# Products for eight tokens in two-bank PSUM tiles, and lists with fewer VectorE steps, in a hybrid decoder layer with expert retrieval

## The chip, the cores and the metric

The kernel runs on one core of one Trainium2 chip. A core has TensorE (PE, matmuls), VectorE (DVE), ScalarE (ACT), GpSimd (POOL) and SyncE (SP), each with its own queue of instructions that it works through in order, and 16 DMA engines that fill on-chip memory (SBUF). TensorE writes to PSUM, eight banks here, which VectorE and ScalarE read. The metric is the time of one execution on the device in microseconds.

## The reference

One decoder layer over 512 prompt tokens and 32 sample tokens, width 1024: retention and a convolution share a projection in and a projection out, a layer norm follows, and then an expert retrieval (PEER), whose sum is added to the tokens ahead of a second layer norm. The retrieval is what the change touches:

```python
q = (xb @ w_query).reshape(PEER_BLOCK, PEER_HEADS, PEER_DQ)          # 8 heads, 256
q1, q2 = q[..., : PEER_DQ // 2], q[..., PEER_DQ // 2:]
s1 = jnp.einsum('phd,hkd->phk', q1, sub_keys_1)                       # 128 keys
s2 = jnp.einsum('phd,hkd->phk', q2, sub_keys_2)
v1, i1 = lax.top_k(s1, PEER_TOPK)                                     # 16
v2, i2 = lax.top_k(s2, PEER_TOPK)
cand = (v1[..., :, None] + v2[..., None, :]).reshape(PEER_BLOCK, PEER_HEADS, PEER_TOPK * PEER_TOPK)
sv, ci = lax.top_k(cand, PEER_TOPK)
e1 = jnp.take_along_axis(i1, ci // PEER_TOPK, axis=-1)
e2 = jnp.take_along_axis(i2, ci % PEER_TOPK, axis=-1)
idx = e1 * N_KEYS + e2
gate = jax.nn.softmax(sv.astype(jnp.float32), axis=-1).astype(xb.dtype)
u = jnp.take(peer_u, idx, axis=0)                                     # of 16384 experts
act = jax.nn.gelu(jnp.einsum('phkd,pd->phk', u, xb), approximate=False)
vv = jnp.take(peer_v, idx, axis=0)
return jnp.einsum('phk,phkd->pd', gate * act, vv)
```

So each token has 8 x 16 = 128 experts with a gate each. The matrices are float32.

## The kernel before

The retrieval is computed in two ways. For 288 tokens (the first 128 prompt tokens, the 32 samples, a block b of 128) the rows of u and v of each expert are gathered from memory by GpSimd's indirect DMAs, one expert per token at a time, into a tile of 128 x 2048. Of each gathered tile VectorE takes the dot with the token (line 697), ScalarE the Gelu (708) and the product with the gate (709), and VectorE accumulates (714). For the last 256 tokens (ND) all experts are computed densely, for one "key" e after another, 128 experts each: the scores sp of a key are 8 matmuls (`scores_of`, line 973; the trace lists each twice, so 16), their Gelu goes to a place in the tiles Ga, Gb, Gc and Gd, and this is multiplied by the gate weights of the tokens, which are zero but for their 128 experts.

These gate weights are built on chip. A list (`retrieve`) finds for some heads of up to 128 tokens the 16 best experts E and their gates: VectorE sorts (`top16`), converts positions (622, 623), adds candidates (628), sorts again, finds the experts by comparison (644 to 651), and lines 653 to 658 are the softmax, whose exp alone is on ScalarE and needs its own table there. There are 14 lists: five for the first 128 tokens, four for the 256 dense tokens, one for the samples ("s") and four for block b.

For the dense tokens experts and gates are transposed (line 1021, ScalarE copies 1025 to 1029, VectorE 1031 and 1033 split the gate into two float16 parts gtT). `build` then makes for each group of 8 tokens (TB) an A that marks the first sub-key (odd groups on VectorE, 1070; even ones on ScalarE, 1076 and 1077) and a B that has the gate at the second (VectorE, M at 1080 and twice B at 1084), and multiplies them on TensorE (1100), two matmuls a token, into a PSUM tile of 4 tokens x 96 keys. `first_keys` takes each such tile out: for keys whose Gelu is there already VectorE multiplies it in place (1129), for the others ScalarE copies it (1132). Keys 52 to 95 have their scores ahead of the build (`early_keys`, Gelu at 1005). The other 52 (`s_stage`) are scored between the products, with Gelus at 1113 and 1115 and a product on VectorE for the tokens that have been built (1116). After the tokens of S_AT, 4 in this kernel, list "s" starts behind the last eviction.

Then the V stage: for each key 4 matmuls (1159; 8 in the trace) of the weights with the key's rows of v into the accumulators pB, four PSUM banks. Before it the `residual` (537) puts the scaled tokens into these banks, 16 matmuls (32 in the trace). The last 32 keys are scored, built and multiplied within the V stage. The gathers, the lists of block b, and the norms of the finished blocks run on the other engines all along.

PSUM: the early scores have four banks (psp, banks 4 to 7), the transposes and query products the other four (pq, banks 0 to 3). When both are released, the pool pdn takes two banks for "mm" (products) and two for sp, and pacc the four of pB.

The order of each engine's instructions is set by the tile framework's scheduler, which simulates the program; `behind` adds an order between two instructions. Keys' rows ("uv") are loaded by SyncE into four buffers (UV).

## Time and profile before

| | us |
|---|---|
| median of 3 runs | 1465.27 (1461.19 to 1468.07) |
| the profiled execution | 1464.26 |
| its span | 1462.5 |
| TensorE busy | 1402.5 (96%) |
| VectorE busy | 1166.1 (80%) |
| ScalarE busy | 500.6 (34%) |
| GpSimd busy | 420.1 (29%) |
| DMA engines, mean rate | 347 GB/s, 506.80 MB in all |

The profile is of one execution; the span runs from its first to its last instruction. "Busy" adds the instructions' durations without overlaps. A matmul's end is modelled. A row of a timeline has its start from the span's begin, its length, the engine, the line of the kernel, the operation, what it writes and reads with shapes, how many instructions of the kind followed one another (x), and in brackets how long the engine was idle before it and what is taken to have released it. PEclk is the share of TensorE's full clock that was granted.

### The profile page before, as it was taken

The numbers are of one execution on the slowest core, as the hardware profiler recorded it, in microseconds if no ns is written. First come the engines' busy times: TensorE is split into PE (matmuls) and PEld (weight loads), VectorE is DVE, ScalarE is ACT, GpSimd is POOL, SyncE is SP. The second block draws the span as 40 slices with busy tenths as digits, with TensorE's granted clock in tenths as the row PEclk, the third lists the DMA queues.
The fourth block names the chain that finished last, engine by engine and source line by source line (L and its number), as shares of the span: only waits on it lengthen the run. The fifth ranks groups of instructions, "written<-read, shape, count | busy, mean of one in ns | idle before, by whom it ended". The sixth has DMA issues, their size and how long they took to land. (4 is left out here: it accounts for less than half of the span.)

```text
span 1462.5 us, 19654 instructions
## 1 busy us (share of the span) xinstructions
PE 1402.5 (96%) x6666; PEld 960.8 (66%) x6666; DVE 1166.1 (80%) x2874; ACT 500.6 (34%) x1498; POOL 420.1 (29%) x405
## 2 busy tenths in 40 slices
PE   8898899999999999989999999999999999999997
PEld 7878455568767578878888884444444666666443
DVE  5828878988858989999899996878879766666666
ACT  1423673345122232333545542113655111111111
POOL 1172134333432322232222311333322222222330
PEclk9999999999999999999999999999999999999999
DMA  9849489978989689999999966999999999999995
GB/s 349 307 174 373 171 286 370 413 291 293 347 357 375 223 315 389 364 395 348 328 395 361 347 252 227 423 422 402 386 354 365 398 416 405 418 404 405 410 407 196
DMA packets 100403, 506.80 MB, mean 347 GB/s; under 512 B 10279, under 2 KB 21287, under 8 KB 57413
## 3 DMA queue, kind: packets, MB, share of 16 engines
q0 software_dynamic: 43392, 309.32, 54.1%
q1 hardware_dynamic: 52157, 190.10, 34.0%
q10 hardware_dynamic: 4752, 6.11, 1.2%
q8 instruction: 53, 0.87, 0.2%
q14 instruction: 49, 0.40, 0.1%
HBM read 500.12 MB, written 5.80 MB: 346 GB/s over the span
## 5 line engine op out<-in xcount | busy, mean ns | idle before, releaser
L973 PE MATMUL sp<-x1T,uv 128*128 128x256 f32 x2048 | 463.8, 383 | 0.4 <-ACT Gc L1115 0.2
L973 PEld LDWEIGHTS sp<-x1T,uv 128*128 128x128 f32 x2048 | 386.3, 191 | 65.0 <-issue 11.9
L714 DVE SCALAR_TENSOR_TENSOR acc<-g,wgt,acc 128x1024 f32<-128x1024 f32 x252 | 323.1, 1282 | 69.6 <-ACT wgt L709 68.8
L697 DVE SCALAR_TENSOR_TENSOR g<-g,x 128x1024 f32<-128x1024 f32 x255 | 310.7, 1220 | 64.5 <-DMA g<-in_uv_dram,Ib 41.2
L708 ACT ACTIVATE act<-act 128x1 f32<-128x1 f32 x288 | 57.7, 202 | 593.9 <-DVE g L697 522.3
L691 POOL DMA_INDIRECT g<-in_uv_dram,Ib x126 | 147.1, 1167 | 383.3 <-PE pB L1159 136.9
L691 POOL DMA_INDIRECT g<-in_uv_dram,I x104 | 134.3, 1291 | 318.7 <-DVE acc L714 187.2
L1159 PE MATMUL pB<-uv,Ga 128*128 128x512 f32 x352 | 158.1, 594 | 0.0
L235 PE MATMUL mm<-x1T,w 128*128 128x384 f32 (+1 forms) x448 | 153.6, 501 | 0.0
L235 PEld LDWEIGHTS mm<-x1T,w 128*128 128x128 f32 x448 | 85.1, 192 | 64.1 <-issue 32.6
L1159 PE MATMUL pB<-uv,Gb 128*128 128x512 f32 x256 | 115.6, 606 | 2.3 <-DVE Gb L1129 1.9
L1159 PEld LDWEIGHTS pB<-uv,Ga 128*128 128x128 f32 x352 | 66.1, 190 | 67.5 <-issue 66.0
L1159 PE MATMUL pB<-uv,Gd 128*128 128x512 f32 x256 | 110.0, 592 | 0.0
L1159 PEld LDWEIGHTS pB<-uv,Gb 128*128 128x128 f32 x256 | 47.8, 192 | 67.3 <-issue 52.6
L1159 PEld LDWEIGHTS pB<-uv,Gd 128*128 128x128 f32 x256 | 48.6, 190 | 60.8 <-issue 59.3
L1076 ACT ACTIVATE A<-row,e1T 128x128 f16<-128x128 bf16 x256 | 78.5, 389 | 18.9 <-PE mm L1100 14.6
L1159 PE MATMUL pB<-uv,Gc 128*128 128x512 f32 x160 | 72.2, 600 | 0.4 <-DMA uv<-in_uv_dram 0.4
L235 PE MATMUL mm<-g,w 128*128 128x160 f32 (+1 forms) x512 | 68.0, 294 | 0.0
L235 PEld LDWEIGHTS mm<-g,w 128*128 128x128 f32 x512 | 67.1, 198 | 0.2 <-ACT score L607 0.2
L1113 ACT ACTIVATE W<-sp 128x256 f32<-128x256 f32 (+26 forms) x84 | 26.7, 318 | 118.0 <-PE sp L973 102.6
L1100 PEld LDWEIGHTS <-A 128*128 128x128 f16 x1024 | 43.5, 97 | 31.3 <-issue 12.4
L691 POOL DMA_INDIRECT g<-in_uv_dram,Is x25 | 34.5, 1378 | 80.9 <-DVE acc L714 27.2
(317 smaller groups left out, 1713.6 us busy)
## 6 DMA issues: line engine op xcount, KB each, us to landing
uv<-in_ut_dram SPq DMA_DIRECT2D x128, 512.0 KB
uv<-in_uv_dram SPq DMA_DIRECT2D x128, 512.0 KB
w<-in_w_in_dram SPq DMA_DIRECT2D x18, 1024.0 KB
w<-in_w_query_dram SPq DMA_DIRECT2D x15, 1024.0 KB
w<-in_w_out_dram SPq DMA_DIRECT2D x7, 1024.0 KB
ln<-in_ln_g_dram POOLq DMA_DIRECT2D x5, 512.0 KB
ln<-in_ln_b_dram POOLq DMA_DIRECT2D x5, 512.0 KB
g<-in_uv_dram,Ib POOLq DMA_INDIRECT x126
```

The costliest lines, as they stand in the source:

```text
L235: T.matmul(p[:, :n], w[m // 2][:, k, (m % 2) * 128:(m % 2 + 1) * 128], xT[:, k, c0:c0 + n], start=(k == 0), stop=(k == 7))
L691: fetch = G.indirect_dma_start(out=t, out_offset=None, in_=a["uv"], in_offset=bass.IndirectOffsetOnAxis(ap=idx[:, k:k + 1], axis=0))
L697: dot = V.scalar_tensor_tensor(t[:, :D], t[:, :D], 1.0, x1, op0=OP.mult, op1=OP.mult, accum_out=act[:, 0:1])
L708: S.activation(act[:, 1:2], act[:, 0:1], AF.Gelu)
L714: V.scalar_tensor_tensor(acc, v, wgt, acc, op0=OP.mult, op1=OP.add)
L973: mm = T.matmul(sp[:, i], u[:, k], x1T[:, k, NG2:], start=(k == 0), stop=(k == 7), skip_group_check=True)
L1076: S.activation(A[:, t], row, AF.Abs, bias=e1T[:, t1 + t:t1 + t + 1])
L1100: mm = T.matmul(pt[:, t % nt], A[t % TB], B[:, q, t % TB // 2, :, t % 2], start=(q == 0), stop=(q == 1))
L1113: S.activation(W[:, :n], sp[:, :n], AF.Gelu)
L1159: return [T.matmul(pB[b][q], W[:, b * 128:(b + 1) * 128], vt[:, q * 512:(q + 1) * 512], start=False, stop=(e == NK - 1), skip_group_check= ...
```

## The change

The lists: positions are converted and multiplied by 1 or 128 in one VectorE instruction, with a small constant tile. The candidates' positions are converted to int16 on ScalarE. The softmax loses the subtraction and the sum on VectorE: ScalarE copies the negated maximum, and computes one exp per head with this as its bias and the sum as a second output. The reciprocal and the product with it stay on VectorE.

The build: a PSUM tile has 8 tokens x 128 places (two banks), of which 96 are used, and three such tiles form the pool pbd. The scores get two banks of their own, psc. Each tile is taken out once, so for 8 tokens in one instruction per range of keys; S_AT becomes 8. The pool of the accumulators pB, and the pool pdn which the last 32 keys' products use, are opened when pbd is closed, after `first_keys`; the residual stands there too.

```diff
@@ -41,7 +41,7 @@
 TURN = (90, 92)
-S_AT = 4
+S_AT = 8
 EG = (32, 20, 44, 32)
@@ -203,6 +203,9 @@
     G.iota(row, pattern=[[1, NK]], base=0, channel_multiplier=0, allow_small_or_imprecise_dtypes=True)
+    unit_k = per.tile([128, 2], F32, name="unit_k")
+    G.memset(unit_k[:, 0:1], 1.0)
+    G.memset(unit_k[:, 1:2], float(NK))
     mhalf = per.tile([128, 1], F32, name="mhalf")
@@ -619,8 +622,8 @@
                     later(first)
-        V.tensor_copy(fi[:n], iu[:n])
-        V.tensor_scalar(fi[:n, :, 1], fi[:n, :, 1], float(NK), None, op0=OP.mult)
+        V.tensor_tensor(fi[:n], iu[:n],
+                        unit_k[:n].unsqueeze(1).unsqueeze(3).to_broadcast([n, nh, 2, TK]), op=OP.mult)
         cand = pick("cand", [128, 2, nh, NCAND], bufs=1)
@@ -634,7 +637,7 @@
         ci = pick("ci", [128, nh, NCAND], I16, bufs=1)
-        V.tensor_copy(ci[:n], cand[:n, 1])
+        S.activation(ci[:n], cand[:n, 1], AF.Copy)
         pf = pick("pf", [128, nh, TK, 2], BF)
@@ -649,11 +652,11 @@
             V.tensor_reduce(E[:n, e0 + j:e0 + j + m], oh[:, :, :, 0:14], axis=AX.X, op=OP.add)
-        ex = pick("ex", [128, nh, TK])
-        V.tensor_sub(ex[:n], sv[:n], sv[:n, :, 0:1].to_broadcast([n, nh, TK]))
-        S.activation(ex[:n], ex[:n], AF.Exp)
-        sm = pick("sm", [128, nh])
-        V.tensor_reduce(sm[:n], ex[:n], axis=AX.X, op=OP.add)
+        ex, sm = pick("ex", [128, nh, TK]), pick("sm", [128, 2, nh])
+        S.activation(sm[:n, 1], sv[:n, :, 0], AF.Copy, scale=-1.0)
+        for j in range(nh):
+            S.activation(ex[:n, j], sv[:n, j], AF.Exp, bias=sm[:n, 1, j:j + 1], accum_out=sm[:n, 0, j:j + 1])
+        sm = sm[:, 0]
         V.reciprocal(sm[:n], sm[:n])
@@ -1045,16 +1048,12 @@
-    pdn = ctx.enter_context(tc.tile_pool(name="pdn", bufs=2, space=PSUM, reuse_waits="tile"))
-    psp[:] = [pdn]
+    psp[:] = [ctx.enter_context(tc.tile_pool(name="psc", bufs=2, space=PSUM, reuse_waits="tile"))]
+    pbs = ExitStack()
+    pdn = [pbs.enter_context(tc.tile_pool(name="pbd", bufs=3, space=PSUM, reuse_waits="tile"))]
     sel[:] = [bsel, True]
...
     gc = ctx.enter_context(tc.tile_pool(name="gc", bufs=1, reuse_waits="tile"))
-    pacc = ctx.enter_context(tc.tile_pool(name="pacc", bufs=1, space=PSUM, reuse_waits="tile"))
-    pB = [[pacc.tile([128, 512], F32, name=f"pB{b}{q}") for q in range(2)] for b in range(2)]
-    for b in range(2):
-        for q in range(2):
-            residual(pB[b][q], x1T, range(q * 4, q * 4 + 4), NG2 + b * 128)
     GW[1] = gc.tile([128, EG[1], ND], F32, name="Gc")
@@ -1094,7 +1093,7 @@
                 if t % nt == 0:
-                    pt = pdn.tile([128, nt, ne], F32, name="mm")
+                    pt = pdn[0].tile([128, nt, ne if ahead else 128], F32, name="mm")[:, :, :ne]
                 A, B = ready[t // TB]
@@ -1119,8 +1118,8 @@
         with tc.tile_pool(name="bt", bufs=2, reuse_waits="tile") as bt:
-            done, units = 0, ND // 4
-            for pt, ts, mm in build(bt, 0, E0S[3], 4):
+            done, units = 0, ND // TB
+            for pt, ts, mm in build(bt, 0, E0S[3], TB):
                 part = lambda e0, e1: pt[:, :, e0:e1].rearrange("p t e -> p e t")
@@ -1130,7 +1129,7 @@
                         S.activation(to(e0, e1), part(e0, e1), AF.Copy, scale=1.0 / GS)
-                while done < E0S[2] * (ts.stop // 4) // units:
+                while done < E0S[2] * (ts.stop // TB) // units:
                     s_stage(done, ts.stop)
@@ -1251,6 +1250,13 @@
     fence.append(first_keys())
+    pbs.close()
+    pdn[0] = ctx.enter_context(tc.tile_pool(name="pdn", bufs=2, space=PSUM, reuse_waits="tile"))
+    pacc = ctx.enter_context(tc.tile_pool(name="pacc", bufs=1, space=PSUM, reuse_waits="tile"))
+    pB = [[pacc.tile([128, 512], F32, name=f"pB{b}{q}") for q in range(2)] for b in range(2)]
+    for b in range(2):
+        for q in range(2):
+            residual(pB[b][q], x1T, range(q * 4, q * 4 + 4), NG2 + b * 128)
     gx2.append(ctx.enter_context(tc.tile_pool(name="gx2", bufs=1, reuse_waits="tile")))
```

The scheduler orders the engines anew. TensorE at the build's start, before (`mm<-cst_89` are the second transposes, `sp` the scores of a key, `mm<-B,A` the products with their weight loads):

```order
L1021 MATMUL mm<-cst_89,e_4215 128x128
L1021 MATMUL mm<-cst_89,eg 128x128 x2
L973 MATMUL sp<-x1T,uv 128x256 x8
L1100 LDWEIGHTS A
L1100 MATMUL mm<-B,A 128x96
```

and now:

```order
L1024 MATMUL mm<-cst_89,e_4215 128x128
L1024 MATMUL mm<-cst_89,eg 128x128 x2
L976 MATMUL sp<-x1T,uv 128x256 x32
L1099 LDWEIGHTS A
L1099 MATMUL mm<-B,A 128x96
```

Four keys' scores stand ahead of the first product in place of one; behind it come the 32 products of the first two groups of 8 tokens, where there were 16 and three more keys.

ScalarE at the same place, before (`Ga<-sp` with 512 columns is the Gelu of a pair of early scores, `act` and `wgt` belong to gathered rows, `Gb<-mm` and `Gc<-mm` take products out):

```order
L1005 ACTIVATE Ga<-sp 128x512
L1025 ACTIVATE gr<-mm 128x128
L1027 ACTIVATE e1T<-mm 128x128
L1028 ACTIVATE e1H<-mm 128x128
L1029 ACTIVATE e2T<-mm 128x128
L708 ACTIVATE act<-act 128x1
L709 ACTIVATE wgt<-act,GT_132 128x1
L1132 ACTIVATE Gb<-mm 128x32x4
L1132 ACTIVATE Gc<-mm 128x20x4
```

and now:

```order
L1008 ACTIVATE Ga<-sp 128x512
L711 ACTIVATE act<-act 128x1
L712 ACTIVATE wgt<-act,GT_135 128x1
L711 ACTIVATE act<-act 128x1
L712 ACTIVATE wgt<-act,GT_135 128x1
L1008 ACTIVATE Ga<-sp 128x512
L1131 ACTIVATE Gb<-mm 128x32x8
L1131 ACTIVATE Gc<-mm 128x20x8
L1075 ACTIVATE A<-row,e1T 128x128 x7
```

The last Gelu of the early scores stood behind the first products' evictions; it now stands ahead of them, behind the Gelus of two gathered rows.

TensorE at the build's end, before (`pB` with `uv` are the V stage's products):

```order
L1100 MATMUL mm<-B,A 128x96
L1159 MATMUL pB_4296<-uv,Gb 128x512
L1159 MATMUL pB_4297<-uv,Gb 128x512
L1100 LDWEIGHTS A
L1100 MATMUL mm<-B,A 128x96
```

and now:

```order
L1099 LDWEIGHTS A
L1099 MATMUL mm<-B,A 128x96
L976 MATMUL sp<-x1T,uv 128x256 x32
L540 MATMUL pB_6809<-scaled,x1T 128x128 x4
L540 MATMUL pB_6810<-scaled,x1T 128x128 x4
L540 MATMUL pB_6811<-scaled,x1T 128x128 x4
L540 MATMUL pB_6812<-scaled,x1T 128x128 x4
L1158 MATMUL pB_6809<-uv,Gb 128x512
```

Products of the V stage were woven into the last groups; now the last products, four keys' scores, the residual and the V stage follow one another. On VectorE the order has 74 evictions from the first gtT cast to the last eviction of Ga, where it had 149, and 403 instructions in all, where it had 521; a layer norm of the sample tokens, the three sums over their parts and half of one list of block b now stand behind that eviction.

## Rows read from the trace of the kernel before

**Rows 1.** Windows: window, length, PE, PEld, DVE, ACT, POOL busy, PEclk, DMA share, GB/s
```profile
646.00:891.00 245.00, 232.81 (x1453) 198.51 (x1453) 233.34 (x594) 122.25 (x466) 64.22 (x51) 0.99 0.88 330
891.00:1462.00 571.00, 563.20 (x2032) 299.95 (x2030) 408.61 (x776) 145.90 (x457) 150.11 (x130) 0.99 0.96 384
```

**Rows 2.** Timeline, TensorE: start us, us, line, operation, count, idle before
```profile
655.04 1.44 PE L1100 MATMUL mm<-B,A 128*128 128x96 f16 x16 [6.69 <-DVE g L697]
```

**Rows 3.** Timeline, ScalarE, ahead of the first products
```profile
652.65 1.04 ACT L1077 ACTIVATE A<-A 128x1024 f16<-128x1024 f16 x1
653.59 0.28 ACT L709 ACTIVATE wgt<-act,GT 128x1 f32<-128x1 f32 x1
653.78 0.57 ACT L1005 ACTIVATE Ga<-sp 128x512 f32<-128x512 f32 x1
...
654.72 0.27 ACT L1029 ACTIVATE e2T<-mm 128x128 f16<-128x128 f32 x1
```

**Rows 4.** Waits of TensorE, 645 to 900 us: us in total, times, longest
```profile
PE mm L1100 <- DVE Ga L1129: 3.0, 3, 1.9
```

**Rows 5.** Timeline, TensorE: the residual, and the start of the V stage
```profile
668.00 3.73 PE L537 MATMUL pB<-scaled,x1T 128*128 128x128 f32 x32
...
875.76 5.78 PE L973 MATMUL sp<-x1T,uv 128*128 128x256 f32 x26
881.37 1.88 PE L1159 MATMUL pB<-uv,Gb 128*128 128x512 f32 x4
883.09 0.85 PE L1100 MATMUL mm<-B,A 128*128 128x96 f16 x16
...
890.36 10.12 PE L1159 MATMUL pB<-uv,Gb 128*128 128x512 f32 x19 [1.87 <-DVE Gb L1129]
```

**Rows 6.** Windows behind two idle times, columns as in rows 1
```profile
654.00:658.00 4.00, 2.96 (x20) 2.69 (x20) 3.97 (x8) 1.77 (x8) 1.53 (x1) 0.50 0.99 403
658.00:662.00 4.00, 4.00 (x18) 3.41 (x18) 4.00 (x8) 1.51 (x6) 1.71 (x2) 0.89 0.76 250
...
891.00:893.00 2.00, 2.00 (x4) 0.82 (x3) 2.00 (x12) 1.97 (x3) 0.00 (x0) 0.50 0.04 8
893.00:895.00 2.00, 2.00 (x4) 0.81 (x3) 2.00 (x9) 1.49 (x2) 0.00 (x0) 0.65 0.12 29
```

**Rows 7.** Groups, VectorE, 646 to 891 us: count, busy us, mean ns, idle
```profile
L714 DVE SCALAR_TENSOR_TENSOR acc<-g,wgt,acc 128x1024 f32<-128x1024 f32 x36 | 46.0, 1279 | 2.6 <-ACT wgt L709 2.5
L697 DVE SCALAR_TENSOR_TENSOR g<-g,x 128x1024 f32<-128x1024 f32 x37 | 45.0, 1217 | 4.2 <-DMA g<-in_uv_dram,Is 4.2
L1084 DVE TENSOR_TENSOR B<-M,gtT 128x768 f16<-128x768 f16 x64 | 32.7, 550 | 0.0
```

**Rows 8.** Timeline, VectorE: first gtT cast, last Ga eviction
```profile
646.52 0.22 DVE L1031 CAST gtT<-gr 128x128 f16<-128x128 f32 x1
...
892.63 0.32 DVE L1129 SCALAR_TENSOR_TENSOR Ga<-mm,Ga 128x176 f32<-128x176 f32 x1
```

**Rows 9.** Timeline, VectorE: evictions in a row
```profile
884.49 0.27 DVE L1129 SCALAR_TENSOR_TENSOR Gb<-mm,Gb 128x128 f32<-128x128 f32 x1
884.69 0.20 DVE L1129 SCALAR_TENSOR_TENSOR Gc<-mm,Gc 128x64 f32<-128x64 f32 x1
884.82 0.27 DVE L1129 SCALAR_TENSOR_TENSOR Gb<-mm,Gb 128x128 f32<-128x128 f32 x1
```

**Rows 10.** One line of the lists: count, ns min/median/max, starts, forms
```profile
L637 DVE CAST ci<-cand x14: 171/200/267, 111.5 to 1121.5; 128x100 int16<-128x100 f32 x8, 128x200 int16<-128x200 f32 x4, 128x50 int16<-128x50 f32 x2
```

**Rows 11.** Timeline, ScalarE: exp of a list in the build, next table load
```profile
686.08 0.23 ACT L654 ACTIVATE ex<-ex 128x32 f32<-128x32 f32 x1 [1.38 <-DVE ex L653]
...
687.83 1.28 ACT L1113 ACT_TABLE_LOAD   x1
689.13 0.19 ACT L1113 ACTIVATE W<-sp 128x20 f32<-128x20 f32 x1
```

**Rows 12.** Timeline, VectorE: the reciprocal of that list
```profile
689.35 0.16 DVE L657 RECIPROCAL sm<-sm 128x2 f32<-128x2 f32 x1
```

## The prediction

> **What bounds the kernel now.** I read the table of busy times by stage first [rows 1]. In the last 571 us, the V stage, TensorE is busy for 563.2 and the DMA engines for 0.96: nothing of the change's products or lists can shorten that run of matmuls, it can only start earlier. Between 646 and 891 us, the build, TensorE is busy for 232.8 of 245 us and VectorE for 233.3, ScalarE for 122. TensorE has 12.2 us of idle time there and VectorE 11.7, so the two queues are nearly equal: what TensorE no longer waits for, VectorE must be able to supply.
>
> The waits of TensorE name the idle times. The largest, 6.69 us, stands ahead of the first products [rows 2]. The answer there names a dot of VectorE, but ScalarE's rows say otherwise [rows 3]: the A rows are done at 653.7, and the last copy out of the second transposes, e2T, ends at 654.99, when TensorE starts at 655.04. These copies hold the PSUM bank which the first product tile takes over. Later come 3.0 us on Ga evictions in three pieces [rows 4] and 1.87 us ahead of the V stage's long run [rows 5].
>
> [...] Work at half clock is the 2.96 us busy and about 0.9 more, half of which, 1.9 us, was lost. Behind the 1.87 us it was 0.50 and 0.65: 2.0 and 1.4 us, 1.7 lost.
>
> **Where the V stage starts now.** Its long run begins at 890.36. By the order 16 of its trace matmuls are already done (8 rows in the order, each two in the trace); four take 883.09 - 881.37 = 1.72 us [rows 5], 0.43 each, so 6.9 us. Undivided, it would have begun at 883.5, and with the 1.7 us lost behind the last idle time this is worth 885.2. I compare the changed kernel with this number.
>
> **The change: TensorE's side.** The order now puts scores of four keys where one stood ahead of the products, so three more, of 16 trace matmuls each. TensorE came to its stall at 655.04 - 6.69 = 648.35. Where 26 of these run in a row they take 881.37 - 875.76 = 5.61 us [rows 5], so 16 take 3.45, and three more keys bring it to 658.7. By then A, B and the bank of the copies are there, since the first unit of 8 tokens takes banks 2 and 3 and the copies ended at 655.0. The second, unit 1, follows 0.8 us later, and takes banks 4 and 5, where the last pair of early scores lies. These leave by a Gelu on ScalarE that stands behind the Gelu of a dot which in VectorE's order comes well behind the first gtT cast. Between them stand five dots, five accumulations, one A, three M, four B and six small rows. At the durations of [rows 7], M taken like B at 0.55 and A, with 1024 columns in place of 768, at 0.7: 6.1 + 6.4 + 0.7 + 1.65 + 2.2 + 1.3 = 18.3; rows overlap by some 0.07 each, so 17. From 646.52 [rows 8] the dot ends at about 663.6. Two rows of one column on ScalarE, 0.28 for the second, and the Gelu of 512 columns, 0.57 [rows 3], follow: 1.1 us, with the handovers between the engines some 1.6. Unit 1 starts near 665.2. **The stall is swapped, not removed**: 5.7 us in place of 6.7, with the same loss of clock.
>
> Without any idle time or clock loss TensorE would have come to the V stage at 883.5 - 12.2 - 1.9 = 869.4, residual included, since that is only moved. With the new stall and its clock, 5.7 + 1.9, it comes at 877.0. The 3.0 us of eviction waits I take as gone, since three tiles of 8 tokens are in flight in place of two of 4.
>
> **VectorE's side.** From the first gtT at 646.52 to the end of the last Ga eviction at 892.95 are 246.4 us [rows 8]. Three things leave this stretch. Evictions: by the orders 74 in place of 149, the elements stay. Three in a row start 0.20 and 0.13 us apart for 128 and 64 elements [rows 9], a slope of 0.0011 us an element, so that 0.06 is fixed; 75 x 0.06 = 4.5, at most 4.9 with a line through all 149. Work that moves behind the last eviction: the sample block's three adds of 1024 columns, taken like accumulations at 1.2 us (3.6), one of two layer norms with its residual, about 5 us, and half of a list for the block b, about 5. Between the two orders I price every row by its start-to-start time and get 18.1 us less. With the waits as they are, the last eviction ends at 646.5 + 246.4 - 18.1 = 874.8. The moved work is still done, beside the V stage, where TensorE sets the pace.
>
> Here the added wait comes in. The residual now needs the four banks that the product tiles held, so it stands behind the last evictions, where before it lay at 668.00, early [rows 5]. It takes 3.6 us, so the V stage starts at 878.5, 1.5 us behind TensorE's own 877.0. The clock may fall for that idle time as it did for 1.87 us: I take half of 1.7. Queued behind the residual are all V products; nothing else on TensorE.
>
> **Lists.** Each of 14 lists loses five VectorE rows, all near the 0.2 us of the cast [rows 10], and gets one in return. Start to start that is about 0.37 us a list, 5 in all, of which 3.6 before the build. ScalarE gets two copies and up to three more exps, some 0.7 us a list. The new cost is a wait: the reciprocal now needs negation, table load and exps, all after the sorted values. In the rows of a list in the build, the load took 1.28 us and the next Gelu ran 0.02 us after it, an exp took 0.23 [rows 11], and the reciprocal came 3 us after the exp [rows 12]; the chain is some 2.2 us. By the new order three of the first nine lists have less VectorE work than that as cover, 0.25, 1.3 and 1.8 us, together 3.3 short; for one of those, two exps stand on either side of another Gelu, so a second load of 1.28 is added. So the 3.6 us are given back, and I count the lead of VectorE at the build's start as nothing; it can lie between +3.6 and -3. In the build the reciprocal of one list may wait; I leave VectorE's waits there at their 11.7 us in all [rows 1], since dots for the sample tokens come later in its queue and wait less for their rows.
>
> [...]
>
> **The sum.** 885.2 - 878.5 - 0.85 = 5.8 us gained, from 1464.26 of the profiled execution 1458.5. The median of the runs, 1465.27, is 1.0 above that execution; I forecast **1459 us**. For the stages ahead of the build I take no change, with 3 us either way: their idle times hang on single rows of VectorE and ScalarE which the lists shift.
>
> **Rivals.**
> 1. The start is free. VectorE is 3.6 us ahead, the Gelu of the last pair is early, and TensorE comes near its 869.4. VectorE's path is then 874.8 - 3.6 + 3.6 = 874.8, a gain of 10.4 and no clock loss: 1454, with a floor at 885.2 - 869.4 = 15.8, 1448.5. For it: ScalarE has half its time free. Against it: the five dots ahead of that Gelu. Chance 0.20.
> 2. Evictions have a larger fixed share: they may block VectorE for more than their start-to-start share when they alternate with other rows. At twice 4.5, VectorE ends at 870.3, TensorE's 877.0 bounds, gain 8.2: 1456. Against it: the starts 0.13 apart [rows 9]. Chance 0.05. [...]
> 3. The change doesn't do what it says: the larger tiles free VectorE, but the residual and the new bank order hold TensorE for as long as before. With both queues so near, 5 us of new waits on VectorE are enough: 1464 to 1466. Chance 0.13.
> 4. Slower: the softmax on ScalarE holds VectorE in the lists. ScalarE's queue is in order, and A rows, Gelus and evictions stand around the exps; where they lie between load and last exp, the reciprocal waits 2.6 us in each list. Five of them (four for the 256 dense tokens, one in the build) delay the evictions by 13 us: 1459 + 13 = 1472. It decides from a chain of about 5 us, against covers of 1.8 to 4. Against it: the chain is 2.2 us where the queue is free, and six of nine covers exceed it. Chance 0.12.
>
> **How the numbers follow.** My forecast, the swap, has 0.50, with its own range of 1455 to 1464. The bound of what can be told from no change is 0.5%, 7.3 us, so faster is below 1457.9: rivals 1 and 2 and a quarter of the forecast's own, 0.37. Slower is above 1472.6 or close to it: rival 4, 0.12. The rest, 0.51, is the same. The range 1449 to 1470 leaves out a little of rival 1 and most of rival 4.
>
> **What would show it.** Right: the first products at about 658.7, an idle time of 4 to 6 us ahead of unit 1 with ScalarE's Gelu as its end, half clock behind it, no further eviction waits, the V stage's first product near 878.5 behind a residual that waits for the last Ga eviction, VectorE's evictions 74 rows. Wrong: no idle time at unit 1 (rival 1); last eviction ahead of 872 (rival 2) or behind 880 (rivals 3 and 4); reciprocals that wait over 2 us each for ScalarE (rival 4); a V stage in which TensorE waits for rows or DMA, which I price at nothing because it waits hardly at all there now.

## The result, and the profile after

The changed kernel takes 1478.6 us (median of 6 runs, 1475.0 to 1480.1) against 1461.5 of the kernel before in the same comparison: a ratio of 1.0096, 95% interval 1.0077 to 1.0114. It is slower by some 14 us, where I forecast 6 us faster; the time lies outside my range. (The medians are 17 us apart. The ratio, taken over all runs, gives 14, and every "Measured" below is such a ratio to the kernel before; 0.001 is 1.5 us.) The profiled execution after has a span of 1477.2 us, 14.7 longer than before.

The stages first. The windows of the changed kernel are cut where its build and its V stage begin; columns as in [rows 1]:

```profile
0.00:660.00 660.00, 614.61 (x3191) 468.43 (x3192) 520.80 (x1470) 243.14 (x633) 210.06 (x227) 0.96 0.83 314
660.00:895.00 235.00, 222.79 (x1427) 194.41 (x1426) 222.18 (x499) 115.69 (x418) 63.55 (x49) 0.98 0.90 339
895.00:1477.00 582.00, 571.71 (x2052) 301.96 (x2050) 413.85 (x777) 149.67 (x477) 159.10 (x132) 1.00 0.95 378
```

The build's start, which lay at 646, lies at 660: most of the time is lost ahead of the stage that the forecast worked on. TensorE's timeline around the first products shows it (start, length, operation, count, idle before):

```profile
657.11 0.38 PE L1024 MATMUL mm<-cst,eg 128*128 128x128 f32 x2
657.32 13.98 PE L976 MATMUL sp<-x1T,uv 128*128 128x256 f32 x64
671.14 0.85 PE L1099 MATMUL mm<-B,A 128*128 128x96 f16 x16
681.93 1.44 PE L1099 MATMUL mm<-B,A 128*128 128x96 f16 x16 [9.93 <-ACT Ga L1008]
...
877.78 14.04 PE L976 MATMUL sp<-x1T,uv 128*128 128x256 f32 x64
891.66 3.73 PE L540 MATMUL pB<-scaled,x1T 128*128 128x128 f32 x32
895.23 5.32 PE L1158 MATMUL pB<-uv,Gb 128*128 128x512 f32 x12
```

The second transposes end at 657.5. The first of these rows was at 644.51 before, and at 636.89 in a run with the build's edits alone (e2 below), whose TensorE, VectorE, ScalarE and GpSimd have the order of the kernel before up to there:

```profile
644.51 0.38 PE L1021 MATMUL mm<-cst,eg 128*128 128x128 f32 x2
```

```profile
636.89 0.38 PE L1021 MATMUL mm<-cst,eg 128*128 128x128 f32 x2
```

So they ended at 644.9, and 12.6 us of the 14.7 are lost ahead of them. With the second profile as base it would be 20.2: two profiles of one order lie 7.6 us apart here, and what follows on stages is no more exact than that. Half of the 12.6 is idle time of TensorE, half is the same work taking longer, at a lower clock. Its windows up to the last transposes, before and after, have the same 3177 rows, 39.5 us idle and then 45.4, 605.1 us busy and then 611.8, and a mean granted clock of 0.97 and 0.96 of the full one:

```profile
0.00:644.60 644.60, 605.07 (x3177) 461.11 (x3178) 522.74 (x1505) 231.81 (x573) 205.55 (x224) 0.97 0.85 320
```

```profile
0.00:657.20 657.20, 611.81 (x3177) 465.94 (x3178) 518.74 (x1468) 241.49 (x626) 208.62 (x226) 0.96 0.83 314
```

Behind the transposes things go as described: four keys' scores, one unit of products, then the idle time at unit 1, ended by a Gelu of the last early scores, then at the end four keys' scores, the residual and the V stage in one piece. From there to the V stage the changed kernel needs 237.7 us; before, to the point 885.2 that the prediction worked out, it was 240.3. So in these two profiles the build gained 2.6 us, not 5.8.

The 9.93 us have the cause that was named, and are longer. ScalarE's and VectorE's timelines there:

```profile
680.86 0.20 ACT L711 ACTIVATE act<-act 128x1 f32<-128x1 f32 x1 [4.47 <-DVE ln L700]
681.10 0.29 ACT L712 ACTIVATE wgt<-act,GT 128x1 f32<-128x1 f32 x1
681.30 0.58 ACT L1008 ACTIVATE Ga<-sp 128x512 f32<-128x512 f32 x1
```

```profile
676.42 1.28 DVE L717 SCALAR_TENSOR_TENSOR acc<-g,wgt,acc 128x1024 f32<-128x1024 f32 x1 [0.60 <-ACT wgt L712]
679.60 1.23 DVE L700 SCALAR_TENSOR_TENSOR ln<-ln,x 128x1024 f32<-128x1024 f32 x1 [1.89 <-DMA ln<-in_uv_dram,I]
```

The Gelu waits behind the Gelu of a dot, and that dot waited 1.89 us for its gathered rows and behind accumulations that waited 0.60 us each. Behind the idle time the clock is low, as in [rows 6]:

```profile
680.00:684.00 4.00, 2.07 (x18) 1.98 (x18) 3.40 (x6) 2.05 (x7) 0.99 (x2) 0.50 1.02 424
684.00:688.00 4.00, 4.00 (x14) 3.24 (x14) 4.00 (x14) 3.07 (x10) 0.15 (x1) 0.67 0.92 324
```

The granted clock is 0.50 and 0.67 of the full one in these two windows, so of 2.1 and 4.0 us of work some 1.0 and 1.3 were lost, 2.3 in all, for which I had 1.9 from the clocks of 0.50 and 0.89 in [rows 6]. The waits on Ga evictions [rows 4] and the idle time ahead of the V stage [rows 5] are gone, as forecast: from 640 us on, the largest waits of TensorE (total us, times, longest) are

```profile
PE mm L1099 <- ACT Ga L1008: 9.9, 1, 9.9
PE sp L976 <- ACT Gb L1114: 1.9, 2, 1.6
PE sp L976 <- DMA uv<-in_ut_dram: 1.1, 3, 0.8
```

The second lies in the build, at 749 and 762 us; the third lies in the V stage, which I had priced at no loss.

### The profile page after: what moved, and what is told of

Read it like the earlier page. It is cut to its first block, busy times and chain, and to the rows that moved or that the text cites. A ratio compares the mean times of both kernels' runs of the same rounds, so it can differ in the third digit from the quotient of the medians.

```text
span 1477.2 us, 19531 instructions
## 1 busy us (share of the span) xinstructions
PE 1409.1 (95%) x6666; PEld 964.8 (65%) x6666; DVE 1156.8 (78%) x2743; ACT 508.5 (34%) x1527; POOL 432.7 (29%) x407
## 4 chain that ended last, share of the span: by engine, by line
PE 51%; DVE 21%; DMA 13%; ACT 6%; issue 5%; POOL 3%; SPq 0%; DVEq 0%; ACTq 0%; POOLq 0%
PE pB L1158 23%; PE sp L976 14%; PE mm L238 7%; DVE acc L717 6%; DMA g<-in_uv_dram,I 4%; DVE g L700 4%; DMA g<-in_uv_dram,Ib 3%; PE mm L930 2%; PE mm L1099 2%; DMA ln<-in_uv_dram,I 2%; DMA uv<-in_ut_dram 2%; PE mm L553 1%; ACT blk L304 1%; DVE ln L700 1%; ACT A L1075 1%
## 5 line engine op out<-in xcount | busy, mean ns | idle before, releaser
L694 POOL DMA_INDIRECT g<-in_uv_dram,Ib x126 | 154.5, 1226 | 376.2 <-PE pB L1158 135.5
L694 POOL DMA_INDIRECT g<-in_uv_dram,I x104 | 137.9, 1326 | 342.9 <-DVE acc L717 188.9
L1075 ACT ACTIVATE A<-row,e1T 128x128 f16<-128x128 bf16 x256 | 78.2, 391 | 15.7 <-PE mm L1099 15.7
L1112 ACT ACTIVATE W<-sp 128x256 f32<-128x256 f32 (+25 forms) x84 | 26.7, 317 | 115.6 <-PE sp L976 115.5
```

The lines of the kernel that those rows point to most:

```text
L694: fetch = G.indirect_dma_start(out=t, out_offset=None, in_=a["uv"], in_offset=bass.IndirectOffsetOnAxis(ap=idx[:, k:k + 1], axis=0))
L1075: S.activation(A[:, t], row, AF.Abs, bias=e1T[:, t1 + t:t1 + t + 1])
L1112: S.activation(W[:, :n], sp[:, :n], AF.Gelu)
```

## The build's edits and the lists' edits apart

The theory: the build's edits gain, and the lists' edits cost ahead of the build, where I had counted them as nothing. The rival: the new PSUM pools cost.

**e1: All list edits, build as before** (fi, ci and softmax of `retrieve`, as in the diff above).

> The kernel before with the list edits only: one-step conversion, candidates and softmax on ScalarE; build, tiles and residual as before. Theory A (the loss lies ahead of the build and comes with the list edits): the second transposes of the dense tokens come near 657 us in place of 644.4, with the idle time at the retention states near 9.6 us and more half-clock stretches ahead of 400 us; time 1470 to 1476. Theory B (the build edits lose it, the front moved for another reason): the transposes come at 644 to 647 and the time is 1459 to 1464.

Measured: 1.0156 (1.0131 to 1.0180), 23 us slower, with a median of 1486, above both ranges. In its profile the second transposes end at 653.2, 8.3 us later than before, and the rest of its 19.5 us stands behind them. So theory A has the edits right and the place only in part.

**e2: The build's edits alone** (`retrieve` as before, all other lines of the diff).

> The kernel before with the build edits only: tiles for 8 tokens, the accumulators' banks and the residual behind them; lists as before. Theory A: the front is as before (transposes at 644.4), the stall ahead of the second unit of products is 6 to 10 us, and from the transposes to the V stage it is 2 to 3 us shorter than before: 1457 to 1462. Theory B: 1470 or more, with the loss behind 645 us.

Measured: 0.9951 (0.9931 to 0.9972), 7 us faster, with a median of 1455.6, under the range of theory A. The two ratios multiply to 1.0106, close to the 1.0096 of both. The build's edits are worth about what the forecast had for everything, and the lists take three times that away. Where the build's edits gain is not shown: of the 8.9 us by which this profile is shorter than the one before, 7.6 lie ahead of the last transposes, in the same order of rows, and 1.3 behind them.

**e3: The scores' two banks at the other end of PSUM**, so that unit 1 does not inherit the banks of the last early scores:

```diff
-    psp[:] = [ctx.enter_context(tc.tile_pool(name="psc", bufs=2, space=PSUM, reuse_waits="tile"))]
+    psp[:] = [ctx.enter_context(tc.tile_pool(name="psc", bufs=2, space=PSUM, side="right", reuse_waits="tile"))]
```

> As the build edits alone, but the two banks of the scores are taken from the other end of PSUM, so that the first two product tiles lie in the four banks that the transposes and query products leave (ScalarE copies done near 655) and only the third tile lies over banks of the early scores. If the second unit's stall was the Gelu of the last early scores, it falls from 6 to 10 us to under 2, the clock does not fall there, and the time is 5 to 10 us under the build edits alone: 1449 to 1455. If VectorE's queue ends the build anyway, the stall goes but the residual waits longer: 1456 to 1461.

Measured: 0.9956 (0.9936 to 0.9977), the same as with the banks as they were. TensorE's waits in the build, first with the build's edits alone, then with the banks moved:

```profile
PE mm L1096 <- ACT Ga L1005: 9.8, 1, 9.8
```

```profile
PE mm L1096 <- DVE B L1080: 6.8, 3, 5.9
PE mm L1096 <- ACT Ga L1005: 2.2, 1, 2.2
```

The stall on the Gelu shrinks from 9.8 to 2.2 us and comes back, 10 us later, as 6.8 us on VectorE's B (0.7 with the banks as they were). So the idle time is what TensorE is ahead of VectorE: when the bank is free, the next wait takes it up.

## Which list edit, and in which lists

**e4: The softmax on ScalarE alone**, on the kernel before:

```diff
-        V.tensor_sub(ex[:n], sv[:n], sv[:n, :, 0:1].to_broadcast([n, nh, TK]))
-        S.activation(ex[:n], ex[:n], AF.Exp)
...
+        S.activation(sm[:n, 1], sv[:n, :, 0], AF.Copy, scale=-1.0)
+        for j in range(nh):
+            S.activation(ex[:n, j], sv[:n, j], AF.Exp, bias=sm[:n, 1, j:j + 1], accum_out=sm[:n, 0, j:j + 1])
```

> The kernel before with one of the list edits only: negation, exps and sums on ScalarE, one exp per head; conversion and candidates' copy on VectorE as before. If of the list edits it is the softmax's chain on ScalarE that costs the front (reciprocals and what stands behind them wait for it), the time is 1468 to 1475 and VectorE waits over 1.5 us at several reciprocals. If the front is lost to the changed order of rows in general, it can be anything between 1458 and 1470, without waits at the reciprocals.

Measured: 1.0105 (1.0079 to 1.0130). One reciprocal waits long, 6.8 us at 168. But the transposes end at 643.7 in this profile, as before, and the loss that it shows stands behind them: the order puts no scores ahead of the first products, and TensorE is idle there for 11.9 us in place of 6.69. (This execution took 1473.6 us, the shortest of the four.)

**e5: The changed kernel with the old softmax** (the same edit taken back).

> The changed kernel with the softmax as before (subtraction and sum on VectorE, one exp on ScalarE); the build, the one-step conversion and the candidates on ScalarE as changed. If the softmax alone is what costs, the time is that of the build edits alone or a little less, 1452 to 1458. If the two other list edits, or the new order of rows that any list edit brings, cost the front as well, 1462 to 1470.

Measured: 0.9998 (0.9981 to 1.0014). So the softmax costs 14 to 15 us on either base, and the conversion and the candidates about 7 more against the build's edits alone.

**e6: The negation on VectorE**, the rest as changed:

```diff
-        S.activation(sm[:n, 1], sv[:n, :, 0], AF.Copy, scale=-1.0)
+        V.tensor_scalar(sm[:n, 1], sv[:n, :, 0], -1.0, None, op0=OP.mult)
```

> The changed kernel with one row moved: the negated maximum is computed on VectorE, exps and sums stay on ScalarE. Then no ScalarE row that waits for the sorted values stands ahead of the exps' table load, so the load can run before they are there, as it did in the kernel before. If the load behind the negation is what makes the reciprocals wait (6.2 us in 4 waits ahead of 680 us), the waits fall under 2 us and the time to 1455 to 1465. If it is the number of rows on ScalarE, or their order, the waits stay over 4 us and the time is 1470 to 1480.

Measured: 1.0097 (1.0074 to 1.0120), no better. The reciprocals' waits for exps fell from 7.4 to 4.8 us over the whole span and the time stayed, within some 3 us. Even the 7.4 us are half of what the softmax costs, and a negation on ScalarE is not needed for the loss.

**e7: The one-step conversion alone**, on the kernel before:

```diff
-        V.tensor_copy(fi[:n], iu[:n])
-        V.tensor_scalar(fi[:n, :, 1], fi[:n, :, 1], float(NK), None, op0=OP.mult)
+        V.tensor_tensor(fi[:n], iu[:n],
+                        unit_k[:n].unsqueeze(1).unsqueeze(3).to_broadcast([n, nh, 2, TK]), op=OP.mult)
```

> The kernel before with the one-step conversion of positions only. Two VectorE rows become one of the larger shape. If rows saved are time saved, 1458 to 1463; if the changed order alone moves the front by several us, it shows here without any new wait for ScalarE: 1465 to 1472.

Measured: 1.0055 (1.0035 to 1.0075). Here 14 VectorE rows are saved, no row waits for an engine for which it did not wait before, and the kernel is 8 us slower.

**e8: The candidates' copy on ScalarE alone** (`V.tensor_copy(ci...)` becomes `S.activation(ci..., AF.Copy)`).

> The kernel before with the candidates' copy on ScalarE only. The copy has two products of VectorE and a wait behind it in every list. If it is harmless, 1458 to 1464; if the one-hot products wait for it, VectorE shows waits for ScalarE at the product with ci, and the time is 1466 to 1472.

Measured: 1.0060 (1.0037 to 1.0083), 9 us slower. VectorE waits nowhere at the product with `ci`, so it is not the wait that I expected. As in e4 the transposes are not late (642.7), and TensorE is idle for longer ahead of the first products, behind another order there. Its longest waits in the build with the softmax alone, then with the candidates alone:

```profile
PE mm L1100 <- ACT e2T L1029: 11.9, 1, 11.9
```

```profile
PE mm L1100 <- ACT e2T L1029: 11.0, 1, 11.0
```

**e9, e10, e12: Early and late lists.** Five lists come in the front (E0, for the first 128 tokens), nine later. First the changed kernel with those five as before, `if E is not E0:` around the three edits; then the converse; then the build's edits with conversion and candidates in the nine later lists alone.

> The changed kernel with the five lists of the first 128 tokens as before; the other nine lists as changed, and the build as changed. TensorE's order is the kernel before's up to the first scores. Theory C (any edit of the first five lists gives the front another order of rows, and that order costs 8 to 13 us): the front is as before, the second transposes come at 636 to 647 us and the time is that of the build edits alone, 1452 to 1460. Theory D (the new rows themselves cost, in every list, above all the softmax on ScalarE): nine of the fourteen lists still have them, and the time is 1466 to 1474.

Measured: 1.0003 (0.9982 to 1.0024), between the two ranges. The transposes end at 640.5, as theory C has it, and 7.6 us more than with the build's edits alone are lost all the same.

> The changed kernel with only the five lists of the first 128 tokens as changed; the other nine as before, the build as changed. Theory C: the whole loss is here, 1470 to 1478. Theory D: some third of it, 1460 to 1466.

Measured: 1.0058 (1.0038 to 1.0077), in the range of theory C: the edits in these five lists cost 15.7 us, give or take 4, against the build's edits alone.

> As the first of these runs, but with the softmax as before in all lists: conversion and candidates changed in the nine later lists, build as changed. If the softmax on ScalarE costs in the later lists too, this is faster than that run by 4 us or more, 1448 to 1454; if not, within 3 us of it.

Measured: 0.9935 (0.9914 to 0.9956), the fastest kernel of the study, with the build's edits alone inside its interval. So conversion and candidates cost nothing in the nine later lists, and some 9 us (e5 against e12) in the five of the front; the softmax costs in both places, 8 to 10 us in the later ones (r4 below, and e9 against e12).

## What the front loses: the rows, or their order

VectorE's time in the front is not short: of the 200 us between 100 and 300 it is busy for 163.8 in the kernel before and 152.7 in the changed one, and where it waits differs. Its waits there for ScalarE's `wgt` and `sg` (total, times, longest), in the kernel before and then with the conversion alone:

```profile
DVE acc L714 <- ACT wgt L709: 6.0, 6, 2.4
DVE u_p L266 <- ACT sg L261: 3.2, 1, 3.2
```

```profile
DVE acc L717 <- ACT wgt L712: 13.7, 6, 5.1
DVE u_p L269 <- ACT sg L264: 4.2, 1, 4.2
```

9.2 us have become 17.9, from 14 rows of 0.2 us. One place of it, on VectorE's timeline near 164 us; before:

```profile
164.26 0.62 DVE L266 SCALAR_TENSOR_TENSOR u_p<-mm,cols,sg 128x384 f32<-128x384 f32 x1 [3.19 <-ACT sg L261]
165.96 1.29 DVE L714 SCALAR_TENSOR_TENSOR acc<-g,wgt,acc 128x1024 f32<-128x1024 f32 x1 [1.08 <-ACT wgt L709]
```

with the conversion alone, where `acc` stands ahead of `u_p`:

```profile
164.63 1.28 DVE L717 SCALAR_TENSOR_TENSOR acc<-g,wgt,acc 128x1024 f32<-128x1024 f32 x1 [4.95 <-ACT wgt L712]
...
167.07 0.61 DVE L269 SCALAR_TENSOR_TENSOR u_p<-mm,cols,sg 128x384 f32<-128x384 f32 x1
```

`u_p` is 2.8 us later though ScalarE's `sg` ended at 162.89, 1.3 us earlier than before. TensorE's waits for the `sg` of line 340 (in the edited kernels 343) up to 640 us go the same way, 2.9 us before, 6.8 with the conversion alone and 7.5 after (longest 1.8, 5.7 and 6.3). These waits do not measure the loss, though. In the changed kernel VectorE's two sum to 13.1 us, less than with the conversion alone, and it is slower. Two waits stand there near the same place, the second on the new chain of the softmax:

```profile
165.60 0.62 DVE L269 SCALAR_TENSOR_TENSOR u_p<-mm,cols,sg 128x384 f32<-128x384 f32 x1 [3.42 <-ACT sg L264]
169.11 0.17 DVE L660 RECIPROCAL sm<-sm 128x2 f32<-128x2 f32 x1 [2.90 <-ACT ex L658]
```

Two theories fit this. O: the scheduler, whose simulation sees other rows, puts all rows in a new order, and that order is worse. R: ScalarE holds VectorE up there (it is busy for 99.7 of the same 200 us before, 98.9 after), so time that VectorE saves returns as a wait, in any order. The first try (e11) gave the kernel before another order with the same rows: `ci` is converted ahead of the second sort.

> The kernel before with two independent lines of the lists exchanged: the cast of the candidates' positions stands ahead of the second sort in place of behind it. The same rows run, none is added, removed, moved to another engine or made longer; only the order in which the scheduler puts them differs, in all lists, in the front most. Theory C: the time moves by 5 us or more, most likely up, 1468 to 1475. If only the new rows cost, it stays at 1460 to 1466.

Measured: 1.0005 (0.9990 to 1.0020). Not every new order costs, then. VectorE waits 12.7 us on the two causes above, between the 9.2 and the 17.9, TensorE 6.4 us for the `sg` of line 340, nearly as long as with the conversion, and the time is that of before. This leaves O and R open, since the order differs from that of the conversion.

The decisive run (r1) keeps the order and changes the rows. The program records each engine's instructions; from a list of the order in the kernel before, each row up to the second transposes is put behind its predecessor:

```diff
+    for e, held_rows in zip((V, S, T), HELD):
+        for k0, k1 in zip(held_rows, held_rows[1:]):
+            behind(e.log[k1], e.log[k0])
```

> The kernel before with only the conversion of positions in one VectorE step (14 rows fewer), as e7_conv_alone, which took 1.0055 of the time before. New: up to the second transposes the remaining rows of VectorE, ScalarE and TensorE are chained in the order that they have in the kernel before, so that the scheduler cannot move them. Theory O (the front pays for the order that the scheduler makes anew once rows change): the loss is gone, 0.998 to 1.001, VectorE's waits for ScalarE in 100 to 300 us back from 20.6 us to 10 to 12, the second transposes at about 642 to 645 us. Theory R (freed VectorE time comes back as waits for a packed ScalarE, whatever the order): 1.004 to 1.006, waits near 20 us.

Measured: 0.9997 (0.9982 to 1.0012), apart from the 1.0055 of the same edit without the list. The waits are those of the kernel before (every row has line 110 here, that of the recorder):

```profile
DVE acc L110 <- ACT wgt L110: 5.3, 6, 1.4
DVE u_p L110 <- ACT sg L110: 3.2, 1, 3.2
```

Behind the transposes, where nothing is held, TensorE, VectorE and GpSimd have the same order in both runs, so the front's order is what differs. In the profiles the transposes end at 646.9 with the conversion alone and at 641.3 here. So O holds for the conversion: its rows cost nothing, the order that came with them costs 8 us, give or take 4. The gain of its saved rows is too small to see.

**r2: All edits, the front held in the order of before** (the rows that both kernels have).

> The changed kernel with all its edits, but up to the second transposes the rows that it shares with the kernel before are chained in that kernel's order (the new ScalarE rows of the lists stand where the scheduler likes). The changed kernel took 1.0096. Theory O: the 17 us of the front go, the 8 us of the nine later lists' softmax and the 8 us that the build gains stay: 0.997 to 1.002, second transposes at 637 to 645 us. Theory R: 1.007 to 1.010, second transposes at 652 to 657 us. In between (about 1.004) if conversion and candidates cost by order and the softmax by its own chain.

Measured: 1.0049 (1.0032 to 1.0067), the case in between. The transposes end at 640.2, as theory O has it; what is left of the loss stands mostly behind them.

**r3: The same with the old softmax.**

> The changed kernel with the softmax as before in all lists (e5_no_softmax: 0.9998) and the front held in the order of the kernel before, as in r2. Theory O: as e12_late_nosoft, in which the five lists of the front were not edited, 0.991 to 0.996. Theory R: 0.998 to 1.001.

Measured: 0.9960 (0.9943 to 0.9977). Holding the order takes 6 us off the kernel without the softmax (0.9998) and 7 off the one with it (1.0096). With the front's order held, the softmax still costs 13 us. Whether its rows cost this or an order is not shown: the hold ends at the transposes, and behind them TensorE's and VectorE's orders differ between r2 and r3 (five keys' scores ahead of the first products in r2, four in r3). The orders of r4 and e2 differ there too, and those of e9 and e12. No run holds that part.

**r4: The softmax in the nine later lists alone**, with the build's edits.

> The build edits (e2_build_alone: 0.9951) and the softmax on ScalarE in the nine later lists alone; conversion, candidates and the five lists of the front as before. If the edits add up, e9 minus e12, 7.9 us: 1.000 to 1.002, with the loss behind 400 us. If the softmax costs only together with the other list edits, 0.994 to 0.997.

Measured: 1.0010 (0.9997 to 1.0023), against 0.9951 without it: 8.6 us, as e9 and e12 had it. In the profiles its build is 5.2 us longer than with the build's edits alone, and its V stage 4.1. The longest new wait stands in the V stage. TensorE, then ScalarE, in this kernel:

```profile
1002.51 0.96 PE L1103 MATMUL mm<-B,A 128*128 128x32 f16 x32
1003.32 7.11 PE L1162 MATMUL pB<-uv,Gc 128*128 128x512 f32 x16
1018.00 1.03 PE L1103 MATMUL mm<-B,A 128*128 128x32 f16 x32 [7.57 <-ACT A L1080]
```

```profile
1007.59 0.30 ACT L716 ACTIVATE wgt<-act,GTb 128x1 f32<-128x1 f32 x1
1009.69 0.20 ACT L654 ACTIVATE sm<-sv 128x2 f32<-128x2 f32 x1 [1.80 <-DVE sv L592]
1010.68 1.28 ACT L656 ACT_TABLE_LOAD   x1 [0.79 <-DVE sv L595]
1011.98 0.31 ACT L656 ACTIVATE ex<-sv,sm 128x16 f32<-128x16 f32 x1
1012.19 0.18 ACT L656 ACTIVATION_READ_ACCUMULATOR ex<-sv,sm 128x1 f32 x1
1012.29 2.43 ACT L1079 ACTIVATE A<-row,e1T 128x128 f16<-128x128 bf16 x8
1014.62 0.57 ACT L1151 ACTIVATE Gd<-mm 128x512 f32<-128x512 f32 x1
1015.10 0.29 ACT L656 ACTIVATE ex<-sv,sm 128x16 f32<-128x16 f32 x1
1015.30 0.19 ACT L656 ACTIVATION_READ_ACCUMULATOR ex<-sv,sm 128x1 f32 x1
1015.50 1.28 ACT L715 ACT_TABLE_LOAD   x1
1016.80 0.20 ACT L715 ACTIVATE act<-act 128x1 f32<-128x1 f32 x1
1016.91 1.04 ACT L1080 ACTIVATE A<-A 128x1024 f16<-128x1024 f16 x1
```

ScalarE stands for the list's negation and then for its load, because the sorted values are not there yet, and the A of the last 32 keys is queued behind. From the end of `wgt` at 1007.89 to the first row of A are 4.4 us of waits and list rows, and between A's two steps 1.8 more (second exp, load for Gelu, the Gelu); together 6.2 of the 7.57 us that TensorE waits. With the build's edits alone the longest such wait is 0.9 us.

Elsewhere the loss is not in this place. With the same softmax the longest wait for an A is 1.2 us in e9 and 0.4 in the changed kernel; r2 waits 3.7 us, but so does r3 without it. The front, the build and the V stage of r2 are longer than r3's by 4.7, 4.5 and 6.0 us in the profiles, in pieces that I could not name one by one. So the rows above show how the softmax can hold TensorE, and the cause of the 13 us stays open.

## Why the prediction was wrong

The step that failed is the sentence "For the stages ahead of the build I take no change, with 3 us either way", and the one that fed it, that saved VectorE rows and the new wait cancel. I priced rows and covers, which are terms of one list, and no term for what the scheduler does with everything else. The front lost 12.6 us in the profile (20.2 against e2's), and the edits of its five lists cost 15.7 us by the ratios (e10 against e2). By the runs 6 to 8.5 us of this are the new order (r1 against e7, r3 against e5, r2 against the result). For the conversion that is shown, and for the lists together it is what holding the order gave back. About 4 more are left for the softmax there (13 us with the order held, less the 8.6 of the later lists), a difference that is argued and whose cause is open. The softmax in the nine later lists, which I had also counted as nothing in the sum, costs 8.6 us (r4), by rows or by order.

Step by step:

- **TensorE's side of the build**: right in kind. The stall is swapped, its end is the Gelu named, low clock stands behind it, the eviction waits of [rows 4] are gone. The size was off: 9.9 us for 5.7, because I counted the rows between the first gtT cast and the dot at VectorE's pace, without the waits for gathered rows and `wgt`, some 3 us, and because TensorE reached its stall 1.4 us sooner behind the first gtT cast than I had it. The 0.5 us for handovers between the engines was my estimate, from no row; in the rows above 1.10 us pass from the dot's end (680.83) to TensorE's start (681.93), where I had 1.6. The banks' experiment (e3) shows that the stall itself decides little: VectorE's B ends the next ones there, 6.8 us in all.
- **VectorE's side**: 74 evictions stand in the trace's build. From the first gtT to the end of the last Ga eviction are 228.7 us (660.42 to 889.14), and I had 228.3. But this path did not set the start of the V stage: TensorE came to the residual only at 891.66, behind four keys' scores, and ran it without idle time, so the wait of 1.5 us and the 0.85 for its clock did not come. That evictions between other rows have twice the fixed share, as rival 2 has it, no run shows: 68 evictions of the changed kernel's build that a row of another kind followed without a wait took, start to start, 0.002 us less in the mean than the line through [rows 9] gives; the last one of Ga (888.62, 352 columns) took 0.43 us, for 0.45. TensorE needed 237.7 us from the transposes to the V stage, where I had 232.1 for it. With the lists as before the build's edits gain 7 us (e2), near the 5.8 that I had for the sum; as most of it stands in the front of that profile, this does not confirm the working.
- **Lists**: wrong in sign. 0.2 us a row was right, and the rows saved did not decide the time.
- **Where the wait is**: I looked for VectorE's reciprocal behind ScalarE. The waits exist, 2.90 us at 169 and 7.4 in all, and moving the negation away shortened them without a gain (e6). The other direction I did not price: ScalarE waiting for VectorE's sorted values with A, evictions and Gelus queued behind it. That is the shape of the 7.57 us in r4.
- **Rival 4** (slower by the softmax, 1472, 0.12) had the sign and a part of the cause; its five waits of 2.6 us on reciprocals are not what the trace shows, which has seven, 7.4 us in all. With its negation and its sums on ScalarE the softmax cost 15 us (e4), although ScalarE is busy for 34% of the span. The candidates' copy to ScalarE cost 9 us, and the conversion, which stays on VectorE, cost 8. For the conversion the order is the reason; for the candidates it is the likelier one, since no wait for the copy shows; for the softmax it was not tested behind the transposes.
- **V stage unchanged**: off by 4.7 us (from 885.2 to the span's end at 1462.5 before, from 895.2 to 1477.2 after). TensorE is idle for 3.2 us there, against 0.9 before; 1.1 of it are the waits for uv rows shown above. The other 2.4 are longer busy time and are not explained.

The account, with the ratios taken times 1465: build's edits -7; order of the front +7; softmax in the front +4; softmax in the later lists +9; sum +13, measured +14. Each term carries 2 to 4 us of uncertainty, so that the sum comes close is in part luck: with e10's 15.7 for the front in place of 7 and 4 it would be near 17. By place it does not close either. In r4 and e9 the loss of the later lists' softmax stands behind the transposes, 9.4 and 6.4 us against e2's profile; in the changed kernel only 3.4 more than in e2 stand there, and 20.2 ahead.

## What to carry to other kernels

Where a scheduler orders the program, an edit of small rows is two edits: the rows, and a new order of all that stands near them. Give the order a term with bounds of its own (here 0.55% for one edit that saves 14 rows of 0.2 us, and nothing in another case), and tell the two apart by holding the old order. Moving the softmax's chain to ScalarE added waits in both directions here: VectorE's of 2.90 us for the exps (at 169 us in the changed kernel), and ScalarE's of 1.80 and 0.79 us for the sorted values (r4), with an A behind them for which TensorE waited 7.57 us. Ask what is queued behind the first row of the chain, not only who needs its last.

## What the runs showed of the hardware

An exp with a sum as its second output leaves two rows: 0.29 to 0.31 us, and an ACTIVATION_READ_ACCUMULATOR of 0.18 to 0.20 which overlaps it by about 0.1. One exp for 32 columns took 0.23 [rows 11]; two for 16 columns each take 0.7 from first start to last end (168.39 to 169.08 in the changed kernel), so the exp split by head, with its sums and its bias operand, takes three times as long. What each of the three costs was not taken apart.

A single profile's milestones scatter more than the edits are worth: the kernel before and the build's edits alone have the same order of TensorE, VectorE, ScalarE and GpSimd up to the second transposes, and ended them at 644.9 and 637.3 us in their profiles (638.4 in e3, with the same order again). The ratios, not single traces, carry the verdicts above.
